# Sparse attention two heads ahead, its old keys and values fetched at once, all mixer weights loaded in 8 KB pairs, and the second tile's picks later

## The chip, the cores and the metric

The kernel runs on one core of a Trainium2 chip. The metric is the device time of one execution in microseconds (us). The engines are named as in the profile: PE is TensorE's matmul stream and PEld its weight loads, DVE is VectorE, ACT is ScalarE, POOL is GpSimd, SP is SyncE, which issues most of the DMAs.

## What is computed

One decoder block on 512 tokens of 1024 channels, all in 32-bit floats. Two token mixers run side by side on the same normed input `h`: a gated linear attention (GLA, 4 heads) and a sparse attention (DSA, 8 heads, each query keeping a part of the keys that an indexer chooses). Each has an output matrix, and a sigmoid gate by channel merges them ahead of a common output matrix. After that comes PEER, a mixer over 16,384 experts of which each token uses 8 x 16. In short:

```python
h = rmsnorm(x, norm1_g) * (1 + scale1) + shift1
gq, gk, gv, gr, glow, dq, dkv, iq, ik, iw, za, zb = split(h @ w_in)
ya = gla(gq, gk, gv, gr, glow) @ w_branch_a
yb = dsa(dq, dkv, iq, ik, iw, w_uk, w_uv) @ w_branch_b
x = x + gate1 * ((sigmoid(za) * ya + sigmoid(zb) * yb) @ w_out)
h2 = rmsnorm(x, norm2_g) * (1 + scale2) + shift2
x = x + gate2 * peer(h2)        # sum over 128 chosen experts: gelu(h2 . u_e) * gate_e * v_e
out = rmsnorm(x, final_norm_g)
```

The shifts, scales and gates come from `silu(c) @ w_ada + b_ada`, the conditioning vector.

## The kernel before

**Two halves of the tokens.** Tokens are handled in two halves of 256 (two tiles of 128 each). `mixing(0)` computes the mixers of the first half with each weight split into a high and a low part (`split`, L115: ACT casts the high part, DVE subtracts to get the low one) and three matmuls for each product; `mixing(1)` computes the second half with plain 32-bit matmuls (`plain`), one for each product at four times the time. In each half the order is: projections of the indexer and of the latent, four GLA heads (`project`, `mix_head`), the GLA's output matrix with its gate (`branch(0)`), eight DSA heads (`dsa_project`, `soften`, `attend`), `branch(1)`, the output matrix (`w_o`), and the norm that gives `h2`. After each half `scores` multiplies by PEER's query matrix and finds the best keys.

**Weights.** `raw` (L157) brings a weight of 128 x 1024 elements (4 KB to a partition, 512 KB) by a DMA on SP into one of `NRAW = 3` slots. In the second half, where no split parts are kept, the two 8 KB slots `w2` serve as four more. A DMA into a slot waits until PE (plain) or DVE (split) has finished with what lies there, and everything behind it on SP waits too. `projT` (L190) uses one weight for a 128 x 256 result, `projN` (L197) two for a result laid out the other way.

**DSA.** `dsa_project(hh)` makes the head's queries and, from the latent and the weight `w_ukv`, its keys `kk` and values `vv` of the own 256 tokens; ACT copies them out of PSUM. The first half stores them to `kvd`, one DRAM tile for each head; the second half loads them from there with two DMAs of 128 KB for each head (L603). `soften(hh)` does the logits on PE (L618), adds the position term and finds the maximum on DVE, and exponentiates on ACT; `attend(hh)` transposes the weights (L636), copies them (`pT`), and multiplies by `vv` (L640). The loop goes one head ahead:

```python
        for hh in range(8):
            cur = soft
            if hh < 7:
                soft = soften(hh + 1, *dsa_project(hh + 1))
            attend(hh, *cur, o)
```

**PEER of the first half: the gather.** The experts of tokens 0 to 255 are fetched by index from `rows` on POOL (`gather`, L1026 and after): for tile 0, 64 steps fetch two rows of u for each token and dot them with `h2n` (L1014), 64 steps fetch rows of v and add them up (L1023); for tile 1, 128 steps fetch u and v together. It is a generator that runs in the background: `pump` (L144), called at each weight, advances it at a given rate, so its instructions stand between those of the second half on DVE. At step 40 it runs `pick(1, ...)`, eight steps in which DVE turns the scores of tile 1 into indices.

**PEER of the second half: dense.** For tokens 256 to 511 all experts are computed. `dots_of` multiplies 128 experts' rows of u (`up`, two blocks a load of 1 MB) with `h2`; the first `AHEAD = 48` of these run early. `dense` then goes over 128 blocks `ib` of 128 experts: it splits a tile of v (`vb`, two blocks to a load of 1 MB, three buffers in the pool `dn`) into `vs`, does 24 matmuls of 512 columns into four accumulators, and runs a further `dots_of`. The weights by expert lie in DRAM (`gd`) and come back as `gtile`, in a buffer of `dn` or in the one of `hl`, which the early dots' `up` tiles use. `gathered(0)` and `gathered(1)` finish the gathered tiles (gate, add, norm, out), with `fx` and `fy` in raw slots.

**What sets the order.** The code is recorded, and each engine runs its instructions in the order the recording puts them; SP's DMAs are issued in order as well. Pools reuse buffers in turn, so a tile's load waits for the last reader of the buffer that it takes.

## Time and profile before

| | us |
|---|---|
| median of 3 runs (1849.02 to 1855.12) | 1853.64 |
| the profiled execution | 1861.09 |
| its span | 1859.4 |
| PE busy | 1725.0 (93%) |
| DVE busy | 1432.8 (77%) |
| ACT busy | 719.0 (39%) |
| POOL busy | 540.5 (29%) |

The DMA engines moved 573.33 MB, 308 GB/s over the span; HBM was read for 553.86 MB. In time the stages stand so: start to 44 us; mixing of the first half 44 to 345; its scores to 450; mixing of the second half 450 to 842 (GLA to about 600, `branch(0)` to 660, DSA to 735, `branch(1)` to 776, `w_o` and the norm behind it); scores of the second half to 900; early dots, picks and building of the weights to 1188; dense 1203 to 1845; end 1859. A busy share is read against the stage: idle time of an engine that nobody waits for costs nothing, and an engine that is fully busy in a stage sets its length.

### The profile page before, as it was taken

The numbers are of one execution on the slowest core, as the hardware profiler recorded it, in microseconds if no ns is written. First come the engines' busy times: TensorE is split into PE (matmuls) and PEld (weight loads), VectorE is DVE, ScalarE is ACT, GpSimd is POOL, SyncE is SP. The second block draws the span as 40 slices with busy tenths as digits, with TensorE's granted clock in tenths as the row PEclk, the third lists the DMA queues.
The fourth block names the chain that finished last, engine by engine and source line by source line (L and its number), as shares of the span: only waits on it lengthen the run. The fifth ranks groups of instructions, "written<-read, shape, count | busy, mean of one in ns | idle before, by whom it ended". The sixth has DMA issues, their size and how long they took to land.

```text
span 1859.4 us, 25034 instructions
## 1 busy us (share of the span) xinstructions
PE 1725.0 (93%) x8898; PEld 1466.6 (79%) x8898; DVE 1432.8 (77%) x2985; ACT 719.0 (39%) x1694; POOL 540.5 (29%) x459
## 2 busy tenths in 40 slices
PE   6999999989899988988999789699999999999995
PEld 3888999878667877877778678588888888888874
DVE  5797645348999868757996999388878888788887
ACT  3644465332121134102144778243333434333343
POOL 0012000001454456653431666021222222222220
PEclk9999999989998999998999889899999999999998
DMA  7757556625786799996886999699999999999983
GB/s 289 281 182 272 187 188 213 231 88 204 245 303 237 284 353 387 381 383 233 294 286 222 345 315 367 246 416 401 403 401 404 397 404 412 395 405 410 393 354 122
DMA packets 145279, 573.33 MB, mean 308 GB/s; under 512 B 14449, under 2 KB 41201, under 8 KB 111106
## 3 DMA queue, kind: packets, MB, share of 16 engines
q1 hardware_dynamic: 89858, 303.28, 44.1%
q0 software_dynamic: 55296, 268.46, 37.4%
q8 instruction: 70, 1.15, 0.2%
q14 instruction: 55, 0.45, 0.1%
HBM read 553.86 MB, written 17.83 MB: 307 GB/s over the span
## 4 chain that ended last, share of the span: by engine, by line
issue 33%; PE 29%; DVE 15%; POOL 12%; DMA 8%; ACT 2%; SPq 0%; POOLq 0%; DVEq 0%; another core or an unknown queue 0%; ACTq 0%
POOL grow L1009 11%; PE pmm L184 8%; DMA grow<-rows,ids 4%; DVE grow L1014 3%; PE pmx L184 2%; PE pmm L187 2%; PE pmm L186 2%; PE pmm L188 2%; DVE gacc L1023 2%; DMA gd<-gs 2%; PE psc L898 2%; PE ptr L898 1%; DMA adaw<-w_ada 1%; PE pmx L187 1%; PE pmx L186 1%
## 5 line engine op out<-in xcount | busy, mean ns | idle before, releaser
L1009 POOL DMA_INDIRECT grow<-rows,ids x384 | 482.9, 1258 | 838.8 <-DVE h2n L1023 451.0
L184 PE MATMUL pmm<-h2h,up 128*128 128x256 f32 x2048 | 468.4, 381 | 5.0 <-ACT kept L943 3.1
L184 PEld LDWEIGHTS pmm<-h2h,up 128*128 128x128 f32 x2048 | 385.5, 191 | 59.3 <-ACT kept L943 3.9
L1014 DVE SCALAR_TENSOR_TENSOR grow<-grow,h2n 128x1024 f32<-128x1024 f32 x256 | 310.4, 1219 | 66.5 <-DMA grow<-rows,ids 65.2
L117 DVE TENSOR_TENSOR vs<-vb,vs 128x1024 fp32r<-128x1024 f32 x128 | 156.3, 1221 | 33.1 <-ACT vs L116 32.6
L1023 DVE SCALAR_TENSOR_TENSOR gacc<-grow,dots,gacc 128x1024 f32<-128x1024 f32 x127 | 161.9, 1275 | 15.1 <-DMA grow<-rows,ids 14.0
L1023 DVE SCALAR_TENSOR_TENSOR h2n<-grow,dots,h2n 128x1024 f32<-128x1024 f32 x127 | 162.5, 1280 | 0.0
L116 ACT CAST vs<-vb 128x1024 fp32r<-128x1024 f32 x128 | 133.3, 1042 | 6.0 <-PE ptr L188 3.9
L117 DVE TENSOR_TENSOR w<-raw,w 128x1024 fp32r<-128x1024 f32 x79 | 98.0, 1240 | 45.3 <-ACT w L116 45.0
L186 PE MATMUL psc<-vs,as 128*128 128x512 f32 x256 | 114.6, 454 | 14.5 <-ACT vs L116 14.5
L187 PE MATMUL psc<-vs,as 128*128 128x512 f32 x256 | 102.7, 401 | 10.4 <-DVE vs L117 10.4
L116 ACT CAST w<-raw 128x1024 fp32r<-128x1024 f32 x79 | 82.6, 1046 | 72.9 <-PE pmm L188 32.8
L184 PE MATMUL pmm<-hh,raw 128*128 128x256 f32 x416 | 99.8, 388 | 4.3 <-DVE bsg L689 2.1
L116 ACT CAST as<-kept 128x256 fp32r<-128x256 f32 x128 | 51.3, 403 | 133.7 <-PE ptr L187 128.9
L1062 ACT ACTIVATE dots<-dots 128x1 f32<-128x1 f32 x128 | 25.8, 202 | 198.2 <-DVE grow L1014 198.1
L188 PE MATMUL psc<-vs,as 128*128 128x512 f32 x256 | 101.0, 395 | 0.0
L187 PE MATMUL ptr<-vs,as 128*128 128x512 f32 x256 | 100.6, 393 | 0.0
L188 PE MATMUL ptr<-vs,as 128*128 128x512 f32 x256 | 100.6, 393 | 0.0
L186 PE MATMUL ptr<-vs,as 128*128 128x512 f32 x256 | 99.4, 393 | 0.0
L94 POOL TENSOR_TENSOR rs<-rs,mhalf 128x1 f32<-128x1 f32 (+1 forms) x24 | 18.1, 756 | 266.5 <-DVE rs L93 266.4
L184 PEld LDWEIGHTS pmm<-hh,raw 128*128 128x128 f32 x416 | 77.9, 193 | 17.3 <-DVE bsg L689 2.5
L117 DVE TENSOR_TENSOR as<-kept,as 128x256 fp32r<-128x256 f32 x128 | 53.4, 423 | 47.0 <-ACT as L116 46.9
(377 smaller groups left out, 3527.4 us busy)
## 6 DMA issues: line engine op xcount, KB each, us to landing
up<-u_t SPq DMA_DIRECT2D x64, 1024.0 KB
vb<-v_t SPq DMA_DIRECT2D x64, 1024.0 KB
raw<-wT SPq DMA_DIRECT2D x74, 512.0 KB
adaw<-w_ada SPq DMA_DIRECT2D x20, 1024.0 KB
raw<-wN SPq DMA_DIRECT2D x32, 512.0 KB
raw<-w_br SPq DMA_DIRECT2D x32, 512.0 KB
raw<-w_pq SPq DMA_DIRECT2D x32, 512.0 KB
gd<-gs SPq DMA_DIRECT2D x16, 640.0 KB
```

What stands on the lines that cost most here:

```text
L94: nc.gpsimd.tensor_tensor(dst, dst, mhalf[:, :w], op=ALU.pow)
L116: (hi_eng or nc.scalar.copy)(hi, src)
L117: i = (eng or nc.vector).tensor_tensor(lo, src, hi.bitcast(F32), op=ALU.subtract)
L184: nc.tensor.matmul(dst, a[0], b[0], start=first, stop=last, **kw)
L186: nc.tensor.matmul(dst, a[0], b[0], start=first, stop=False, **kw)
L187: nc.tensor.matmul(dst, a[0], b[1], start=False, stop=False, **kw)
L188: nc.tensor.matmul(dst, a[1], b[0], start=False, stop=last, **kw)
L898: nc.tensor.matmul(p[:, t], pm[:, t4_ + t], qm[:, t4_ + t], start=True, stop=True)
L1009: nc.gpsimd.indirect_dma_start(out=dst, out_offset=None, in_=table, in_offset=bass.IndirectOffsetOnAxis(ap=index[0][:, r:r + 1], axis=0))
L1014: nc.vector.scalar_tensor_tensor(u, u, 1.0, h2n[i], op0=ALU.mult, op1=ALU.mult, accum_out=dots[i][:, r:r + 1])
L1023: nc.vector.scalar_tensor_tensor(gacc, v, w, gacc, op0=ALU.mult, op1=ALU.add)
L1062: nc.scalar.activation(w, w, AF.Gelu)
```

## The change

- `pair` takes the place of `raw`: every weight of the mixers and of PEER's queries comes together with the next one as 128 x 2048 elements (8 KB to a partition, 1 MB) in one DMA. The first half has `NRAW = 2` such slots; the second half takes turns between these and the two of `w2`, four in all. `w_ukv` rides with the query weight of its head (1536 columns). The host lays the weights out in these pairs.
- DSA projects two heads ahead, and `logits` (PE, DVE) is separated from `soften` (ACT), which runs after `attend` of the head before.
- `kvd` is one DRAM tile; the second half's old keys and values come in three DMAs (four heads into the buffer `hl`, twice two heads into `t4`) and are no longer copied into one tile with the new ones, so the logits of a tile are two matmuls.
- Rings: `e` from 7 to 3 buffers, and a new ring `p` of 2 for `neg`, `e2` (`enb` and `eke` together) and `pT`.
- The slabs of `w_ada` lie in rows of 8 KB; those of the first shift come as 4, 2 and 2 to a load.
- In `dense` the tiles of v take turns between the two raw slots and `dn`, which keeps two. `fx` and `fy` of a gathered tile share a raw slot. `dg` takes the buffers of `pq`.
- The picks of tile 1 run at step 72 of the gather, not at step 40.

```diff
-NRAW = 3
+NRAW = 2
-NE = 7
+NE = 3
...
-    kvd = [dr.tile([2, P, TH], F32, name=f"kvd{i}") for i in range(8)]
+    kvd = dr.tile([P, 8, 2, TH], F32, name="kvd")
...
-    def raw(src, width, plain=False):
-
-        if plain and turn[0] % (NRAW + 4) >= NRAW:
-            if not spare:
-                w = wp.tile([P, 2, D], F32, name="raw2", tag="w2", bufs=2)
-                spare.extend([w[:, 0], w[:, 1]])
-            r = spare.pop(0)[:, :width]
-        else:
-            r = wp.tile([P, D], F32, name="raw", bufs=NRAW)[:, :width]
+    def pair(src, width, plain=False):
+
         turn[0] += plain
+        tag, bufs = ("w2", 2) if plain and turn[0] % 2 else ("raw", NRAW)
+        r = wp.tile([P, 2, D], F32, name="raw", tag=tag, bufs=bufs).rearrange("p a c -> p (a c)")[:, :width]
         nc.sync.dma_start(r, src)
-        return r
+        return r[:, 0:D], r[:, D:]
...
         def dsa_project(hh):
+
+            wq, ukv = pair(w_dsa[hh], 1536, plain)
             p = pmm()
-            projT(p[:, :TH], wT[8 + hh], h)
+            projT(p[:, :TH], wq, h)
...
-            for i, t in enumerate((kk, vv)):
-                if hf == 0:
-                    nc.sync.dma_start(kvd[hh][i], t[:, own])
-                else:
-                    nc.sync.dma_start(t[:, 0:TH], kvd[hh][i])
-            return q, kk, vv
+            if hf == 0:
+                nc.sync.dma_start(kvd[:, hh], kv)
+            return q, ([] if hf == 0 else [old[hh]]) + [kv]
...
+        old = []
+        if hf:
+            for h0, n, pool, tag, bufs in ((0, 4, hp, "hl", 1), (4, 2, tp, "t4", 2), (6, 2, tp, "t4", 2)):
+                t = pool.tile([P, n, 2, TH], F32, name="old", tag=tag, bufs=bufs)
+                nc.sync.dma_start(t, kvd[:, h0:h0 + n])
+                old += [t[:, i] for i in range(n)]
...
-        soft = soften(0, *ahead)
+        soft = logits(0, *ahead)
+        soften(*soft)
+        after = dsa_project(1)
         for hh in range(8):
-            cur = soft
+            cur, nxt = soft, after
+            if hh < 6:
+                after = dsa_project(hh + 2)
             if hh < 7:
-                soft = soften(hh + 1, *dsa_project(hh + 1))
+                soft = logits(hh + 1, *nxt)
             attend(hh, *cur, o)
+            if hh < 7:
+                soften(*soft)
...
-                projT(p, wT[16 + 8 * b + d], h)
+                wz, wb = pair(w_bz[b, d], 2 * D, plain)
+                projT(p, wz, h)
...
-                vb = dn.tile([P, 2, D], F32, name="vb", bufs=3)
+                pool, tag, bufs = ((wp, "raw", NRAW), (dn, "vb", 2))[ib // 2 % 2]
+                vb = pool.tile([P, 2, D], F32, name="vb", tag=tag, bufs=bufs)
                 nc.sync.dma_start(vb, v_t[ib // 2])
...
-            if r == 40:
+            if r == 72:
                 for h0 in range(0, 8, HG):
                     yield from pick(1, h0)
```

The diff alone does not tell where the instructions come to stand. SP, from the last product-key weights of the second half to the start of the dense stage, before (the names are the destination and the source of each DMA):

```order
L167 DMA raw_7526<-w_pq 128x1024 x2
L1073 DMA fx<-x2d_90 128x1024
L937 DMA up<-u_t 128x2048 x14
...
L909 DMA gd<-gs 128x10x128
L961 DMA gtile<-gd 128x2048
L1165 DMA fing<-fin_g 128x1024
L1166 DMA gate_9538<-gated_104 128x1024
L961 DMA gtile<-gd 128x2048
L979 DMA vb<-v_t 128x2048
L937 DMA up<-u_t 128x2048
L979 DMA vb<-v_t 128x2048 x2
```

The same stretch of SP in the changed kernel:

```order
L160 DMA raw<-w_pq 128x2048 x4
L1016 DMA vb<-v_t 128x2048
L973 DMA up<-u_t 128x2048
L1016 DMA vb<-v_t 128x2048
L973 DMA up<-u_t 128x2048 x13
...
L946 DMA gd<-gs 128x10x128
L1016 DMA vb<-v_t 128x2048
L997 DMA gtile<-gd 128x2048
L1204 DMA fing<-fin_g 128x1024
L1205 DMA gate_9314<-gated_97 128x1024
L997 DMA gtile<-gd 128x2048
L973 DMA up<-u_t 128x2048
```

Two loads of v now stand right behind the product-key weights (they are those of blocks 0, 1 and 4, 5, in the raw slots) and a third, of blocks 8, 9, ahead of the gate tile; the gate tile, the gain, the gate, the second gate tile and the next u stand as before, and the load of blocks 2, 3 behind them.

SP in the DSA heads of the second half, before (`kk` and `vv` are keys and values, `wT` the queries' weights, `w_ukv` those of keys and values, `w_br` and `wT` at the end the branch's):

```order
L603 DMA kk<-kvd_98 128x256
L167 DMA raw_6412<-wT 128x1024
L603 DMA vv<-kvd_98 128x256
L167 DMA raw_6412<-w_ukv 128x512
L167 DMA raw<-wT 128x1024
L603 DMA kk<-kvd_99 128x256
L167 DMA raw<-w_ukv 128x512
L603 DMA vv<-kvd_99 128x256
```

The same stretch in the changed kernel, with the branches on both sides:

```order
L160 DMA raw<-w_bz 128x2048 x4
L753 DMA xq<-x 128x2x256
L160 DMA raw<-w_bz 128x2048 x4
L160 DMA raw<-w_dsa 128x1536 x7
L160 DMA raw<-w_bz 128x2048 x2
L973 DMA up<-u_t 128x2048
```

The loads of old keys and values are gone from this place; their three DMAs stand behind the first half's attention, its output matrix and the first product-key weights.

PE in the same heads, before (L618 the logits, L636 the transposes, L640 the product with the values, L184 a weight's matmuls, L591 and L596 the new keys and values):

```order
L591 MATMUL pmm<-cT,raw_6412 128x256 x2
L596 MATMUL pmx<-raw_6412,cT 128x128 x4
L618 MATMUL psc<-kk,q 128x384
L618 MATMUL psc<-kk,q 128x512
L636 MATMUL ptr<-ident,wide_lg 128x128 x7
L184 MATMUL pmm<-hh,raw 128x256
L640 MATMUL pout<-pT,vv 128x128 x7
L184 MATMUL pmm<-hh,raw 128x256 x7
```

And in the changed kernel:

```order
L606 MATMUL pmm<-cT,raw 128x256 x2
L611 MATMUL pmx<-raw,cT 128x128 x4
L633 MATMUL psc<-old,q 128x256
L633 MATMUL psc<-kv,q 128x128
L633 MATMUL psc<-old,q 128x256
L633 MATMUL psc<-kv,q 128x256
L655 MATMUL ptr<-ident,wide_lg 128x128 x7
L176 MATMUL pmm<-hh,raw 128x256
```

The places in the row are alike, but the logits at L633 now belong to the head before the one whose keys were made just ahead of them, and are two matmuls for each tile, one on the old keys and one on the new.

## Rows read from the trace of the kernel before

**Rows 1.** Page, part 1: busy time, share, instructions of TensorE and weight loads, VectorE, ScalarE, GpSimd.

```profile
PE 1725.0 (93%) x8898; PEld 1466.6 (79%) x8898; DVE 1432.8 (77%) x2985; ACT 719.0 (39%) x1694; POOL 540.5 (29%) x459
```

**Rows 2.** Busy time by stretch (the columns stand in its first line).

```profile
core 0: us, PE busy (x) PEld busy (x) DVE busy (x) ACT busy (x) POOL busy (x), PEclk, DMA share, GB/s
200.00:345.00 145.00, 144.51 (x1161) 140.39 (x1160) 79.08 (x137) 81.73 (x169) 1.67 (x3) 1.00 0.62 200
560.00:620.00 60.00, 56.32 (x237) 41.84 (x237) 57.73 (x205) 12.65 (x33) 21.35 (x22) 0.91 0.56 192
620.00:680.00 60.00, 58.05 (x290) 49.77 (x289) 41.00 (x81) 11.55 (x27) 34.37 (x29) 1.00 0.94 359
680.00:740.00 60.00, 49.78 (x267) 40.48 (x266) 51.13 (x98) 26.42 (x64) 34.78 (x32) 0.94 1.02 391
740.00:800.00 60.00, 57.09 (x265) 49.35 (x264) 41.67 (x71) 6.94 (x15) 36.41 (x31) 0.97 1.00 386
800.00:842.00 42.00, 32.73 (x137) 27.56 (x136) 24.20 (x39) 4.07 (x16) 19.54 (x16) 0.90 0.99 378
1300.00:1350.00 50.00, 50.00 (x227) 42.65 (x226) 42.60 (x60) 19.95 (x48) 14.66 (x11) 1.00 0.98 404
```

**Rows 3.** Timeline of TensorE, 1186 to 1217 us, at the start of the dense stage.

```profile
1185.67 2.75 PE L184 MATMUL pmm<-h2h,up 128*128 128x256 f32 x12
...
1202.95 1.22 PE L186 MATMUL psc<-vs,as 128*128 128x512 f32 x2 [14.53 <-ACT vs L116]
...
1211.73 3.61 PE L184 MATMUL pmm<-h2h,up 128*128 128x256 f32 x16
1215.00 0.58 PE L186 MATMUL psc<-vs,as 128*128 128x512 f32 x1
```

**Rows 4.** Timeline of SyncE's DMA queue, 1160 to 1215 us.

```profile
1188.46 0.33 SPq L961 DMA_DIRECT2D gtile<-gd  x1
...
1190.47 0.45 SPq L979 DMA_DIRECT2D vb<-v_t  x1
```

**Rows 5.** Waits, 640 to 842 us: us in total, times, longest.

```profile
PE psc L618 <- ACT kk L592: 6.4, 3, 4.0
```

**Rows 6.** DMA, 640 to 842 us: queues (packets, MB, share of 16 engines), issues.

```profile
q0 software_dynamic: 14025, 51.03, 65.6%
q1 hardware_dynamic: 9068, 25.16, 32.6%
...
vv<-kvd SPq DMA_DIRECT2D x7, 128.0 KB
kk<-kvd SPq DMA_DIRECT2D x6, 128.0 KB
```

**Rows 7.** Timeline of SyncE's DMA queue, 700 to 745 us.

```profile
708.12 0.54 SPq L167 DMA_DIRECT2D raw<-wT  x1
...
720.66 0.33 SPq L167 DMA_DIRECT2D raw<-w_br  x1
```

**Rows 8.** DMA, 1240 to 1800 us: the gather's queue.

```profile
q0 software_dynamic: 16190, 117.82, 51.3%
```

**Rows 9.** Timeline of TensorE around 257 us, within one weight's 24 matmuls.

```profile
256.60 0.28 PE L186 MATMUL pmm<-hh,w 128*128 128x256 f32 x1
...
258.27 0.28 PE L188 MATMUL pmm<-hh,w 128*128 128x256 f32 x1
```

**Rows 10.** Instructions that touch raw weights, 200 to 345 us: duration ns min/median/max.

```profile
L116 ACT CAST w<-raw x40: 1035/1049/1056, 199.6 to 341.7; 128x1024 fp32r<-128x1024 f32 x40
L117 DVE TENSOR_TENSOR w<-raw,w x40: 1216/1225/1229, 200.7 to 343.0; 128x1024 fp32r<-128x1024 f32 x40
```

**Rows 11.** Instructions that touch the gather's tiles, 560 to 660 us, and their idle time.

```profile
L1014 DVE SCALAR_TENSOR_TENSOR grow<-grow,h2n x30: 1198/1215/1226, 561.7 to 659.1; 128x1024 f32<-128x1024 f32 x30
...
  DVE eqc L849: 6.8, 2
```

**Rows 12.** Waits of SyncE's DMA queue, 640 to 842 us.

```profile
SPq L167 <- PE pmm L184: 86.2, 16, 11.9
```

150 lines of the change are left out of this document (92 added, 58 removed).

## The prediction

> **What bounds the kernel now.** I read four views in this order: the busy shares, the busy time by stage, the idle time of TensorE (PE) inside the stages, and the DMA queues. PE is busy for 1725.0 of 1859.4 us [rows 1], so all that can be won without doing less arithmetic is some 134 us of idle time, and the stages tell where it lies [rows 2]. In the dense stage (1300 to 1350 us) PE has no idle time at all, 50.00 of 50, while the DMA engines are at 0.98 and 404 GB/s: two resources are full there. In the second half of the first token half (200 to 345) PE is busy 144.51 of 145 with the DMA at only 0.62. From 620 to 842 us, the sparse attention, its branch and the output projection of the second token half, PE is idle for 1.95 + 10.22 + 2.91 + 9.27 = 24.4 us with the DMA at 0.94 to 1.02, some 359 to 391 GB/s. One more hole is not inside a stage but between two: 14.53 us ahead of the first dense block [rows 3]. The change touches all of these places, and the sum is made from them.
>
> The profiled execution took 1861.09 us (span 1859.4), 7.45 us above the median of the runs shown, 1853.64. I make the sum against 1861.09 and carry the result down by 7.45. A measurement of this kernel can tell about 0.3% from no change, 5.6 us.
>
> **The change, part by part.**
>
> *1. The first value tiles of the dense stage.* Today SP issues the gate tile at 1188.46, and the first tile of v follows behind it at 1190.47 [rows 4]; PE ran out of early dots at 1185.67 + 2.75 = 1188.42, and starts on the first cast only at 1202.95 [rows 3]. In the changed order the tiles for blocks 0, 1 and 4, 5 take the two slots of the raw weights and are issued right behind the last product-key weights, hundreds of microseconds earlier, so blocks 0 and 1 follow the early dots at once. But the gate tile takes the buffer that the last early dot reads, so it is still issued at about 1188.4, and behind it on SP stand the final gain, the gate, a second gate tile, the row of u that PE wants after block 1, and the tile for block 2: 1 + 0.5 + 0.5 + 1 MB, then u and v at 1 MB each. At the 404 GB/s of [rows 2], 4.2 million bytes (to the end of u) take 10.4 us and 5.2 million take 13 us, so u lands near 1199 to 1201 and v near 1202 to 1204. PE has two blocks to do, 24 matmuls of 0.227 us, 5.5 us, then waits about 5 to 7 us for u, does the 3.3 us of dots, and begins block 2 at about 1205 to 1206. Today that is 1215.00 [rows 3]. The gain read so is 9 to 10 us. Against it stands that the dense stage is full of transfers: what is moved ahead are 2 MB, and at 404 GB/s they are worth 5.2 us, so if transfers rather than PE set the pace later on, only those 5.2 us are kept. I take 6 us, nearer to the lower figure because both resources are full, with bounds of 4 and 10.
>
> *2. The sparse attention, branch and output projection of the second half.* PE waited 6.4 us in three places for the logits' keys to be copied by ScalarE [rows 5]; projecting two heads ahead puts that copy a whole head earlier, and separating logits from softening does the like for the transposes. The 13 loads of old keys and values go from here [rows 6] to the first half's end, where the DMA share was 0.62; they stood between the weights on SP, and two weights with such loads between them are issued 12.5 us apart [rows 7]. What could swallow the gain is the DMA: if the stage is bound by transfers, only fewer or cheaper transfers shorten it. The 13 loads are 1.7 MB in 1 KB rows; at the queue's price, 32.6% of 16 engines for 202 us over 25.16 MB, which is 41.9 ns per 1000 bytes and engine, they take 4.5 us. The other 23.5 MB become 8 KB rows. The gather's own rows show what that is worth: 51.03 MB in 65.6% here, mostly 4 KB rows, is 41.5 ns per 1000 bytes, and 117.82 MB in 51.3% of 560 us later, 8 KB rows, is 39.0 [rows 6, 8]. That is 6%, or 3.7 us on the weights. Together the transfers fall by 8 us, and PE's idle time by up to 20 of its 24.4 us (the rest is the chain of the norm). I take 8 us, the bound by transfers, with ends of 0 and 20: the stage's DMA share is nearest to full.
>
> The Trainium skill, "DMA: Bandwidth & Descriptors", section Bandwidth, asks for DMAs of at least 1 MiB and gives 78% of peak at 1 MB and 97% at 16 MB, which would make the pairs worth far more than 6%. The rows speak against it: 512 KB loads already run at 391 GB/s when several are in flight, so by the rule some 20 us would be won here, by the rows 8.
>
> *3. All mixer weights in pairs, and two slots in the first half.* The first half had three slots of 4 KB per partition and now has two of 8 KB. A weight takes PE 24 matmuls at 0.12 us, 2.9 us [rows 9], so a pair is 5.8 us. A slot is free when the second of its halves has been split, and the next pair must have landed in time for a cast of 1.05 and a subtraction of 1.23 [rows 10] ahead of PE: 5.8 - 2.3 = 3.5 us are left for 1 MB, which at 404 GB/s takes 2.6 us and at the 200 GB/s of that stage [rows 2] 5.2. So a pair has between 0.9 us to spare and 1.7 us too little. Some 28 pairs (8 of the GLA values, 16 of the branches, 4 of the output) have no other matmuls beside them to cover a delay. If a quarter of them come beside another 1 MB load and lose the middle of the shortfall, 0.4 us, that is 3 us, which I take; the ends are -2 and 11 (28 times 0.4). The gain side is there since a pair halves what SP issues.
>
> *4. The picks of the second tile.* They move from step 40 to step 72 of the gather. In 560 to 620 VectorE is busy 57.73 of 60 us, PE idle 3.68, at a granted clock of 0.91 [rows 2]; the fetches wait 6.8 us for the picks there [rows 11]. The dots that take their place are 1.215 us each [rows 11], 16 of them 19.4 us, so VectorE stays nearly as full, while the picks go to 620 to 680, where VectorE has 19 us free and PE 1.95 us of idle time. What is late next is a PE matmul waiting for a branch's VectorE step behind a pick. I take -2, ends -6 and 3.
>
> *5. The rest.* The index and latent weights in pairs, the first shift's slabs as three loads a half instead of eight, smaller rings for the exponentials and the moved buffers of the last gate and norm: their work lies beside PE in stages where it has 0.5 us idle in 145, or before the first matmul, where the same bytes come. What follows the last dense matmul keeps its steps. Zero; if a cover fails (a slot of the last value tiles waiting for a norm's result), one wait of up to 5 us.
>
> The sum: -6 - 8 + 3 - 2 = -13 us, 1848.1 in the profiled execution's terms, and 1840.7 as a median. **Forecast 1841 us**; its terms' bounds, not all at once, give 1830 to 1850.
>
> **The rivals.**
>
> *Only the dense start helps.* The DMA share of 1.0 in 680 to 800 speaks for it: with weights fewer slots apart the gather simply fills the holes. Parts 1 and 3 alone: -6 + 3 = -3, and half of part 2's transfers, -4: 1846.5. Against it are the waits of PE on a copy, not on a transfer [rows 5].
>
> *The change does not reach the path.* The gate tile still stands ahead of u on SP, block 2 then starts where the transfers let it, and the middle stays as it is, bound by SP's slots (it waited 86.2 us in 16 places for PE to free one [rows 12]). Gain 0 to 3: 1852.
>
> *More than the sum.* All 20 us in part 2, 10 in part 1, part 3 free: -32, 1822. For it: PE's holes are not at places where the DMA was the releaser. Against: the share of 1.0.
>
> *Slower: pairs too large for two slots.* In part 3 the deciding point is a landing 3.5 us after the slot comes free. If SP's issue and the way to memory add 2 us to the 2.6, every one of the 28 uncovered pairs is 1.1 us late, 31 us, and the rest still gives -16: +15, 1869. For it: three slots of 512 KB left PE only 0.5 us idle in 145, so nothing is known of the depth below. Against: DMA share 0.62, most pairs would find the engines free.
>
> *Slower: the gather is starved.* Weights and gather share the engines in 640 to 842, where the gather moves twice the weights' bytes. If the engines take turns by rows, an 8 KB row against a 4 KB row halves what the gather gets while weights queue: a fetch of 524 KB (8 rows on each engine at 41.5 ns per 1000 bytes, 1.4 us) then loses another 1.4 us to the longer rows. With weights queued a quarter of the time, 97 fetches (51.03 MB, [rows 6]) lose 0.35 us each, and VectorE, in order, waits for them: 34 us against the sum's 13, which gives 1875. Against: SP's weights wait for slots, not for engines [rows 12], so their queue is seldom long; hence the smallest chance.
> The Trainium skill, "DMA: Bandwidth & Descriptors", section Queues, rings and completion order, says that an engine goes round-robin between queues by packet, and drains a whole packet before it switches; no row here shows a single turn. By that rule a longer packet of the weights holds the gather back as told above.
>
> **How the numbers follow.** Forecast 0.45, only the dense start 0.18, not on the path 0.10, more than the sum 0.10, two slots too few 0.12, gather starved 0.05. Faster by over 0.3% is below 1848.1: nearly all of the forecast (0.42), half of the dense-start case (0.10) and the tenth above: 0.62. Within 0.3%: the rest of these and the third case, 0.21. Slower: the last two cases, 0.17. The range leaves out the ends of the fastest and the slowest cases: 1818 to 1862.
>
> **What would show it.** Right: block 2's first matmul at 9 to 10 us less than 26.6 us after the last early dot, a PE wait of 5 to 7 us for u between; no wait of over 1 us for a copied key; 680 to 740 with PE at 53 to 56 of 60; PE at 141 or more of 145 from 200 on. Wrong: a cast in the first half that waits for a raw weight by more than 10 us in sum (two slots), VectorE's waits for fetched rows in 640 to 842 well over what they were (starved gather), or the dense blocks losing their full 50 of 50 (the gain of part 1 given back).

## The result, and the profile after

The changed kernel took 1865.91 us (median of 9 runs, 1861.92 to 1874.86), the kernel before 1855.12 in the same comparison (median of 9, 1849.02 to 1864.91). The ratio is 1.0055, with an interval of 1.0034 to 1.0076: the change makes the kernel slower by about 10 us, where 13 us of gain were forecast. The profiled execution took 1868.25 us (span 1866.6), 2.3 us above its median.

PE, in part 1 of the page, did the same work in the same time as before [rows 1]; what grew is idle time, 144.1 us of the span where it was 134.4:

```profile
PE 1722.5 (92%) x8930; PEld 1466.7 (79%) x8930; DVE 1431.0 (77%) x2985; ACT 719.5 (39%) x1694; POOL 543.3 (29%) x459
```

Four of the stretches of [rows 2] in the changed kernel, same columns (us, busy time of PE, PEld, DVE, ACT, POOL, PEclk, DMA share, GB/s), and one at the start of the dense stage. From 663 us on the stages stand some 6 us later than before, so the middle rows cover slightly earlier work:

```profile
200.00:345.00 145.00, 144.42 (x1159) 140.27 (x1158) 78.22 (x134) 79.81 (x163) 1.71 (x3) 1.00 0.58 200
560.00:620.00 60.00, 53.42 (x239) 41.00 (x238) 56.86 (x141) 8.98 (x25) 39.87 (x36) 0.94 0.80 294
620.00:680.00 60.00, 54.44 (x259) 47.21 (x258) 41.30 (x143) 12.38 (x29) 16.85 (x16) 0.94 0.79 294
680.00:740.00 60.00, 50.81 (x293) 45.05 (x292) 44.02 (x83) 24.00 (x60) 30.37 (x26) 0.91 0.83 314
1203.00:1216.00 13.00, 2.78 (x7) 2.17 (x7) 0.43 (x1) 0.61 (x2) 0.00 (x0) 0.70 1.01 414
```

From 200 to 345 nothing is lost, so two slots of 8 KB are enough. From 560 to 680 PE loses 6.5 us more than before, and the DMA share from 620 to 680 falls from 0.94 to 0.79: POOL, which does the fetches, is busy for 39.87 of 60 us before 620 and for 16.85 of 60 behind it.

Fixed windows blur shifted stages, so I cut the execution at starts of PE's own instructions in its timeline: the same matmul by count in each kernel. Each column sums to the span within 0.1 us. The last three columns are experiments told below: the picks put back (e1), the start's slabs loaded one by one (e16), and both (e12).

| stage, us | before | changed | e1 | e16 | e12 |
|---|---|---|---|---|---|
| start to the latent's first matmul | 38.0 | 33.8 | 34.8 | 38.0 | 37.1 |
| the latent's matmuls | 39.4 | 47.5 | 47.6 | 39.2 | 39.2 |
| rest of the first half | 271.6 | 271.2 | 272.5 | 270.7 | 272.4 |
| its scores, GLA of the second half | 265.8 | 260.6 | 266.3 | 265.6 | 260.7 |
| `branch(0)` | 42.2 | 50.5 | 41.9 | 50.4 | 41.8 |
| DSA heads | 72.7 | 64.3 | 65.2 | 64.1 | 65.1 |
| `branch(1)` and half of `w_o` | 93.2 | 102.7 | 101.7 | 100.1 | 101.1 |
| to the last early dot | 365.0 | 366.9 | 367.3 | 362.7 | 362.7 |
| last early dot to dense block 8 | 57.4 | 52.3 | 51.2 | 52.6 | 51.9 |
| block 8 to the last dense matmul | 602.0 | 604.8 | 598.9 | 600.3 | 599.0 |
| end | 12.0 | 12.1 | 11.9 | 12.0 | 12.0 |

Two lines explain nothing and must be set aside. The 5 us that the fourth stage seems to gain lie wholly in the 37.1 us before the GLA, which are 32.1 in some profiles and about 37 in others, of either kernel (e1, with the same code there as the changed kernel, has 37.1). The 2.8 us lost behind block 8 aren't in e1, e16 or e12. One profile is one execution, and such a stage may differ by 5 us from the next one.

What is left: the start loses 3.8 us (77.4 to 81.2), `branch(0)` loses 8.3, the DSA heads gain 8.4 and the stage behind them loses 9.5, the dense start gains 5.1. So the time went to two places that the prediction had at -2 and 0, and one gain was given back at once.

**The start.** PE's timeline, changed kernel (columns: start, us, engine, line, operation, out<-in, count, and idle time before it with its releaser):

```profile
33.76 0.39 PE L178 MATMUL pmx<-hh,w 128*128 128x256 f32 x1 [0.33 <-DVE hh L116]
34.49 0.58 PE L179 MATMUL pmx<-hl,w 128*128 128x256 f32 x1 [0.34 <-DVE hl L117]
34.87 0.42 PE L180 MATMUL pmx<-hh,w 128*128 128x256 f32 x1
35.22 4.72 PE L358 MATMUL pmm<-h2n,sc__118 128*1 128x512 f32 x8
39.77 1.02 PE L359 MATMUL pmm<-adaacc,ones 128*1 128x512 f32 x2
```

The same place of the kernel before:

```profile
32.78 4.45 PE L352 MATMUL pmm<-adae,sc__125 128*1 128x512 f32 x10
37.07 1.02 PE L353 MATMUL pmm<-adaacc,ones 128*1 128x512 f32 x2
38.02 0.39 PE L186 MATMUL pmx<-hh,w 128*128 128x256 f32 x1
```

The last matmuls of the first shift (`pmm<-h2n` now, `pmm<-adae` before) used to stand ahead of the latent's first products. With the slabs in three loads a half, the last one comes as part of a bigger load, its matmuls are recorded three products later, and PE takes its instructions in order: it first does three products whose splits DVE has only just made, and the shift's sum (`adaacc`), on which everything behind `h` waits, starts 2.7 us later (39.77 for 37.07). The shift goes slower, too: eight matmuls take 4.72 us, where the same eight take 3.60 in e12 below.

**`branch(0)`.** PE's timeline, changed kernel, one wait:

```profile
626.73 6.02 PE L176 MATMUL pmx<-hh,raw 128*128 128x256 f32 x16 [5.56 <-DVE yp L716]
```

DVE's timeline of that wait:

```profile
616.76 0.42 DVE L716 SCALAR_TENSOR_TENSOR yp<-bsg,pmm 128x256 f32<-128x256 f32 x1
620.98 1.23 DVE L1052 SCALAR_TENSOR_TENSOR grow<-grow,h2n 128x1024 f32<-128x1024 f32 x1 [3.80 <-DMA grow<-rows,ids]
...
625.11 1.23 DVE L1052 SCALAR_TENSOR_TENSOR grow<-grow,h2n 128x1024 f32<-128x1024 f32 x1 [2.89 <-DMA grow<-rows,ids]
...
626.26 0.42 DVE L716 SCALAR_TENSOR_TENSOR yp<-bsg,pmx 128x256 f32<-128x256 f32 x1
```

It isn't a pick that holds the branch's `yp` back. Where the picks stood there are now gather steps, whose dots wait for fetched rows (3.80 and 2.89 us); `yp` stands behind them on DVE, which is in order, and PE needs the PSUM buffer that `yp` reads. Dots alone don't do it: in `branch(0)` e1 has 22 of them for the changed kernel's 18, none waits longer than 1.6 us, and PE doesn't wait. What is special is that the rows come late: fetches are issued side by side with three 1 MB weights of the branch. Changed kernel, issues from 598 to 610 us, then from 612.5 to 622 (the last number is the median time from issue to landing, in us):

```profile
grow<-rows,ids POOLq DMA_INDIRECT x6, 5.1
```

```profile
grow<-rows,ids POOLq DMA_INDIRECT x6, 11.3
```

The branch loses 8.3 us, more than the wait. The sixteen matmuls behind the wait take 6.02 us where sixteen like them take 3.61 in [rows 3], and the granted clock there is 0.61, a mean over the levels of 1.2 and 2.4 GHz; in `branch(0)` PE is busy for 44.94 us, before for 42.10.

```profile
626.00:633.00 7.00, 6.27 (x18) 5.19 (x19) 4.74 (x11) 0.21 (x1) 3.54 (x4) 0.61 1.02 417
```

The picks, by contrast, wait for no transfer. They now run at 633 to 668 us. POOL's next fetch needs a buffer that a dot behind them must free, so none is issued from 653 to 689:

```profile
689.41 1.69 POOL L1047 DMA_INDIRECT grow<-rows,ids  x1 [36.23 <-DVE grow L1052]
```

From 663.5 to 728 the DMA is at 0.69, in e1 (picks early) at 0.95. First the changed kernel, then e1:

```profile
663.50:728.00 64.50, 59.27 (x344) 52.53 (x343) 40.59 (x84) 25.39 (x63) 23.22 (x20) 0.95 0.69 253
```

```profile
663.00:728.00 65.00, 60.84 (x343) 53.59 (x342) 49.84 (x93) 27.36 (x66) 35.62 (x31) 0.95 0.95 364
```

PE gets through the DSA heads in the same 64 to 65 us either way.

**DSA heads and what follows.** No wait of PE for a copied key is left (it was 6.4 us, [rows 5]). In its place come waits for the softmax. PE, ACT and DVE in the changed kernel around 734 us:

```profile
731.10 1.23 DVE L1052 SCALAR_TENSOR_TENSOR grow<-grow,h2n 128x1024 f32<-128x1024 f32 x1 [0.60 <-DMA grow<-rows,ids]
...
733.53 0.22 DVE L645 RECIPROCAL sm<-sm 128x1 f32<-128x1 f32 x2
```

```profile
733.72 1.23 ACT L646 ACTIVATE wide_lg<-wide_lg,sm 128x384 f32<-128x384 f32 x2 [5.27 <-DVE sm L645]
```

```profile
734.39 0.90 PE L655 MATMUL ptr<-ident,wide_lg 128*128 128x128 f32 x3 [3.96 <-ACT wide_lg L646]
```

The chain reads: transposes wait for the scaled weights, these for a reciprocal, and the reciprocal stands behind the gather's dots on DVE. In `branch(1)` PE waits for `bsg` and `yp` on the same engine. The kernel before had the same three waits, of 2.9, 5.0 and 2.6 us; now they are 9.1, 5.1 and 5.5. The waits of the whole stretch (columns: total us, times, longest), changed kernel, 663 to 830:

```profile
DVE grow L1052 <- DMA grow<-rows,ids: 25.6, 17, 4.7
...
DVE gacc L1061 <- DMA grow<-rows,ids: 9.5, 6, 3.2
...
PE ptr L655 <- ACT wide_lg L646: 9.1, 2, 5.1
...
PE pmm L176 <- DVE yp L719: 5.5, 1, 5.5
...
PE pmm L176 <- DVE bsg L718: 5.1, 3, 2.9
```

Before, 657 to 823:

```profile
DVE grow L1014 <- DMA grow<-rows,ids: 30.1, 25, 5.8
...
DVE gacc L1023 <- DMA grow<-rows,ids: 10.4, 9, 1.9
```

DVE waits less for rows, 35.1 us against 40.5, though for 72 fetches where there were 83; e1, with 82, has 34.7. So the long rows of the weights don't starve the gather.

**The dense start.** SP's queue and then PE in the changed kernel, the places of [rows 4] and [rows 3]:

```profile
1197.77 0.33 SPq L997 DMA_DIRECT2D gtile<-gd  x1
1198.16 0.42 SPq L1204 DMA_DIRECT2D fing<-fin_g  x1
1198.63 0.42 SPq L1205 DMA_DIRECT2D gate<-gated  x1
1199.10 0.64 SPq L997 DMA_DIRECT2D gtile<-gd  x1
1199.78 0.44 SPq L973 DMA_DIRECT2D up<-u_t  x1
```

```profile
1213.42 6.21 PE L176 MATMUL pmm<-h2h,up 128*128 128x256 f32 x16 [10.22 <-DMA up<-u_t]
1219.28 0.58 PE L178 MATMUL psc<-vs,as 128*128 128x512 f32 x1
```

Blocks 0 and 1 follow the early dots without a gap, as predicted, and then PE waits 10.22 us for u behind 3 MB of other loads. The sixteen matmuls behind that wait take 6.21 us, again for 3.61.

### The profile page after: what moved, and what is told of

It is laid out like the page before. It is cut to its first block, busy times and chain, and to the rows that moved or that the text cites. A ratio compares the mean times of both kernels' runs of the same rounds, so it can differ in the third digit from the quotient of the medians.

```text
span 1866.6 us, 24825 instructions
## 1 busy us (share of the span) xinstructions
PE 1722.5 (92%) x8930; PEld 1466.7 (79%) x8930; DVE 1431.0 (77%) x2985; ACT 719.5 (39%) x1694; POOL 543.3 (29%) x459
## 4 chain that ended last, share of the span: by engine, by line
PE 34%; issue 30%; DVE 14%; POOL 11%; DMA 8%; ACT 2%; SPq 0%; POOLq 0%; DVEq 0%; ACTq 0%
PE pmm L176 12%; POOL grow L1047 10%; DMA grow<-rows,ids 5%; DVE grow L1052 3%; PE pmx L176 3%; PE pmm L179 2%; PE pmm L180 2%; PE pmm L178 2%; DMA gd<-gs 2%; PE psc L935 2%; DVE gacc L1061 2%; PE ptr L935 2%; PE pmx L179 1%; PE pmx L180 1%; PE pmx L178 1%
## 5 line engine op out<-in xcount | busy, mean ns | idle before, releaser
L176 PE MATMUL pmm<-h2h,up 128*128 128x256 f32 x2048 | 473.8, 384 | 17.8 <-DMA up<-u_t 13.4
L176 PEld LDWEIGHTS pmm<-h2h,up 128*128 128x128 f32 x2048 | 389.4, 193 | 74.5 <-issue 10.6
L179 PE MATMUL ptr<-vs,as 128*128 128x512 f32 x256 | 100.1, 391 | 0.0
L180 PE MATMUL ptr<-vs,as 128*128 128x512 f32 x256 | 100.1, 391 | 0.0
L116 ACT CAST as<-kept 128x256 fp32r<-128x256 f32 x128 | 51.2, 402 | 125.2 <-PE ptr L179 125.1
```

Source lines behind the costliest of these rows:

```text
L116: (hi_eng or nc.scalar.copy)(hi, src)
L176: nc.tensor.matmul(dst, a[0], b[0], start=first, stop=last, **kw)
L179: nc.tensor.matmul(dst, a[0], b[1], start=False, stop=False, **kw)
L180: nc.tensor.matmul(dst, a[1], b[0], start=False, stop=last, **kw)
```

## The experiments

All ratios are to the kernel before, run on the same chip in the same group, with 95% intervals (about 0.2% to either side). Two ratios of different groups are compared through the kernel before, so their difference is known to some 0.3%, 5 to 6 us.

### e1: the changed kernel with the picks where they were

```diff
-            if r == 72:
+            if r == 40:
```

> The changed kernel with the picks back at step 40 of the gather; all else as changed. Theory A (the picks at step 72 stand on VectorE ahead of the branch's and the attention's own steps): the PE wait of 5.56 us in the first branch goes and with it some 6 to 8 us, so the median falls to about 1858 to 1860. Rival B (the picks cost the same wherever they stand, since the gather halts for them either way): the PE wait goes, but the GLA heads lose as much, and the median stays within 2 us of 1866.

Measured: 0.9989 (0.9969 to 1.0010), median 1861.33 us. With 1.0055 for the whole change, the later picks cost 0.66%, 12 us. In its profile `branch(0)` takes 41.9 us, and between 600 and 640 PE has no wait for `yp`; what waits is POOL, for the picks, as before [rows 11]. In the waits, 600 to 640, the row now reads:

```profile
POOL grow L1047 <- DVE eqc L886: 6.8, 2, 5.8
```

### e4: the kernel before with the later picks alone

```diff
-            if r == 40:
+            if r == 72:
```

> The kernel before with one edit alone, the picks at step 72. Theory A (the late picks cost what the changed kernel loses in the first branch): slower by 5 to 8 us, 1860 to 1863. Rival B (their place does not matter): within 2 us of 1855.

Measured: 1.0020 (0.9998 to 1.0041), 1864.10 us. `branch(0)` takes 50.9 us for 42.2, the same loss as in the changed kernel, and the DSA heads behind it 67.7 for 72.7. So the loss doesn't need the other edits. What the heads gain is lost again in the stage behind them (98.2 us for 93.2), yet the median moves by 0.20%, 4 us, which can't be told from nothing. Why it moves by less than the branch loses stays open.

### e2: softening ahead of `attend`

```diff
-            attend(hh, *cur, o)
             if hh < 7:
                 soften(*soft)
+            attend(hh, *cur, o)
```

> The changed kernel, still two heads ahead, with the softening of a head recorded before the attend of the head before it, not after. Theory A (the reciprocal of the softening stands on VectorE behind dots of the gather that wait for fetched rows, so PE's transposes wait): the PE waits of 5.12 and 3.96 us ahead of the transposes fall below 2 us each, and the median falls by 4 to 9 us to 1857 to 1862. Rival B (the stretch is bound by the fetched rows, and VectorE waits for them wherever the reciprocal stands): the waits move to another PE instruction and the median falls by less than 2 us.

Measured: 1.0047 (1.0027 to 1.0066), 1871.88 us: no gain that can be told from the changed kernel's 1.0055. The DSA heads take 60.6 us instead of 64.3, `branch(1)` and half of `w_o` 107.2 instead of 102.7. The waits ahead of the transposes fall (2.7 us in all, from 9.1), and PE waits for `bsg` instead. A wait removed in the heads comes back behind them, to within a microsecond: these waits don't set the stage's length.

### e3: the dense start's first tiles of v back in `dn`

```diff
-                pool, tag, bufs = ((wp, "raw", NRAW), (dn, "vb", 2))[ib // 2 % 2]
+                pool, tag, bufs = ((dn, "vb", 2), (wp, "raw", NRAW))[ib // 2 % 2]
```

> The changed kernel with the two homes of the value tiles swapped, so that blocks 0, 1 come into the dense stage's own buffer behind the gate tile as in the kernel before, and blocks 2, 3 early. Theory A (the early tiles gain 5 us at the start of the dense stage, and keep them where PE sets the pace): block 0 starts some 14 us after the last early dot, and the median rises by 4 to 6 us to 1870 to 1872. Rival B (the dense stage is bound by its transfers, and what the start gains is given back later): the start is later by 5 us, the end by less than 2.

Measured: 1.0078 (1.0049 to 1.0106), 1876.77 us. From the last early dot to block 8 it takes 58.3 us, as before the change (57.4), and PE's first dense matmul waits again, for a cast of a tile that came behind the gate tile:

```profile
1221.73 1.22 PE L178 MATMUL psc<-vs,as 128*128 128x512 f32 x2 [16.63 <-ACT vs L116]
```

Undoing this part costs 6 us in its stage and 0.23% in the median, which alone is less than two such ratios can tell apart.

### e5: one slot of the first half freed earlier

`one_w`, the GLA's small weights, lies in a raw slot; here it lies elsewhere.

```diff
-        one_w = wp.tile([P, 2, D], F32, name="raw", tag="raw", bufs=NRAW)[:, 0]
+        one_w = t4("one_w")
```

> The changed kernel, where the first half's small weight (the indexer's keys, 4 KB) no longer takes one of the two 8 KB slots but a buffer of its own kind. Theory A (with two slots of 8 KB the pairs ahead of the first GLA head come too late): from the first matmul on a weight to the 63rd of the latent's products the kernel before took 39.4 us and the changed one 47.5; this run takes 42 to 45, and the median falls by 2 to 5 us against the changed kernel's. Rival B (that stretch is set by the casts and by PE's order, not by the slots): 47 to 48 as before, and no change.

Measured: 1.0048 (1.0030 to 1.0066), 1867.14 us. The latent's matmuls start 6.9 us later and take 40.9 us, so they end where they did (81.6 against 81.2). Two slots weren't the cause of the lost start; its end hangs on what comes ahead, the shift. A third slot of 8 KB wasn't tried.

### e6 and e11: a slower gather in the DSA heads

Both with the picks at step 40; `RATE_DSA` is the pace of the gather there. e6:

```diff
-RATE_ADA, RATE_GLA, RATE_DSA, RATE_G, RATE_DENSE = 0.4, 0.75, 0.9, 1.0, 1.05
+RATE_ADA, RATE_GLA, RATE_DSA, RATE_G, RATE_DENSE = 0.4, 0.75, 0.65, 1.0, 1.05
```

> The changed kernel with the picks at step 40 and the gather's rate in the sparse attention, its branch and its output projection lowered from 0.9 to 0.65 steps for a weight. Theory A (from 657 to 823 us the rows that the gather fetches set the pace, so that what the two heads ahead won was given back): those 166 to 167 us shrink to 150 to 158, and the gather's lag comes back as a later end of the dense stage, since its end waits for the gather, so the total moves by less than 10 us either way. Rival B (PE's and ScalarE's own chains set it): the stretch stays at 164 to 168.

Measured: 1.0018 (0.9998 to 1.0037), 1860.45 us. From the end of `branch(0)` to half of `w_o` it takes 138.9 us, where the kernel before takes 165.9, the changed one 167.0 and e1 166.9; PE is busy 141.50 of 143 us. The windows of e6, the middle and the end:

```profile
657.00:800.00 143.00, 141.50 (x763) 124.91 (x762) 98.21 (x189) 42.20 (x106) 68.98 (x60) 1.00 0.97 379
...
1800.00:1856.00 56.00, 8.61 (x36) 6.11 (x34) 44.18 (x64) 11.47 (x36) 14.43 (x12) 0.61 0.59 215
```

With fewer gather steps PE runs through and 28 us are won: about 18 of waiting, and 10 of matmul time, since the same matmuls take 137 us at a granted clock of 1.00 where they take 147 in e1 at 0.95. The gather that was put off ends 46 us after the last dense matmul (1809.9 of a span of 1855.8). So the gather's steps hold the middle, not any one wait inside the heads.

e11 has the pace at 0.84 in the same line.

> The changed kernel with the picks at step 40 and the gather's rate in the sparse attention lowered from 0.9 to 0.84. Theory A (the fetched rows set the pace of 657 to 823 us, and the end has some slack for the gather's last steps): that stretch takes 159 to 163 us instead of 167, about 2.9 us for each step moved to the end, and the end gives back less: 0.995 to 0.998 of the kernel before. Rival B (each step put off costs as much at the end as it saves): 0.998 to 1.000.

Measured: 1.0012 (0.9993 to 1.0031), 1860.14 us: not told apart from e1. Neither pace gains. The stretch takes 166.0 us where 159 to 163 were expected, so a few steps less don't shorten it. By what the gather holds the stage, its bytes or its dots' places on DVE, these runs don't settle: e1 moves 62.2 MB there in 166.9 us and e6 52.9 MB in 138.8, at nearly one rate, but e11 moves 60.2 MB in 166.0 us and the changed kernel 55.4 MB in 167.0.

### e12 and e16: the first shift's slabs one by one

The tiles stay, only each slab is its own DMA again. e16 has this edit alone, e12 has the picks at step 40 as well.

```diff
-                nc.sync.dma_start(t, w_sh[q, :, k:k + len(parts)])
+                for i in range(len(parts)):
+                    nc.sync.dma_start(t[:, i], w_sh[q, :, k + i])
```

> The changed kernel with the picks at step 40 and the first shift's slabs loaded one by one again, eight loads a half, into the same buffers. Theory A (with three loads a half PE's order puts three matmuls of the first weight ahead of the shift's, and PE stands behind them until VectorE has split the first part): the second shift is ready at about 40 us instead of 42.7, and all until the first GLA head is 2 to 3 us earlier, about that of the median too. Rival B (the two slots of 8 KB make the first 80 us late): the shift is earlier, the first GLA head is not.

Measured: 0.9971 (0.9953 to 0.9990), 1850.11 us.

> The changed kernel with the slabs one by one and nothing else. Theory A (the slabs and the picks add up): the latent's 63rd product at 76 to 77 us, and 4 to 6 us under the changed kernel, 1.002 to 1.003 of the kernel before. Rival B (the start's gain is lost in the wait behind the picks): 1.005 as the changed kernel.

Measured: 1.0013 (0.9996 to 1.0029), 1860.57 us. Against the changed kernel the slabs alone are worth 0.42% (e16), against e1 0.18% (e12): 3 to 8 us, with 4 to 6 us in the stage (the latent ends at 77.2 us in e16 for 81.2 in the changed kernel, at 76.3 in e12 for 82.4 in e1). PE's timeline of e12 has the shift first again, its eight matmuls in 3.60 us:

```profile
32.67 3.60 PE L359 MATMUL pmm<-h2n,sc__118 128*1 128x512 f32 x8
36.10 1.02 PE L360 MATMUL pmm<-adaacc,ones 128*1 128x512 f32 x2
37.05 0.39 PE L178 MATMUL pmx<-hh,w 128*128 128x256 f32 x1
```

The picks' cost by this pair is 0.42% (e16 to e12), 8 us. e12 is the changed kernel without its two losses: 0.29% faster than before.

### e13: e12 with one head ahead

The loop of the kernel before, with the rest of the change.

```diff
-        after = dsa_project(1)
         for hh in range(8):
-            cur, nxt = soft, after
-            if hh < 6:
-                after = dsa_project(hh + 2)
-            if hh < 7:
-                soft = logits(hh + 1, *nxt)
-            attend(hh, *cur, o)
+            cur = soft
             if hh < 7:
+                soft = logits(hh + 1, *dsa_project(hh + 1))
                 soften(*soft)
+            attend(hh, *cur, o)
```

> The kernel of e12 (picks at step 40, slabs one by one), with the sparse attention one head ahead and softened at once, as in the kernel before; the old keys and values are still fetched at once. Theory A (from 657 to 823 us the gather's fetched rows set the pace): the loop of the heads takes 72 to 74 us instead of 65, the branch behind it 5 to 8 less, the stretch as a whole 165 to 168, and the time is within 2 us of e12's (0.9971 of the kernel before). Rival B (two heads ahead is worth what it saves in the loop): slower than e12 by 5 to 8 us, 0.999 to 1.001.

Measured: 1.0000 (0.9980 to 1.0021), 1857.43 us. The DSA heads take 75.7 us, the stage behind them 97.7; together 173.4 where e12 has 166.2. The median points the same way (0.29%, 5 us), but the intervals overlap, and kernels with the middle of the kernel before, unchanged, had 165.9 (before, e4), 167.6 (e10), 172.3 (e8) and 173.2 (e15). Whether two heads ahead gains anything isn't settled; it is at most some 10 us.

### e7, e8: all gate tiles later

Ahead of u stood two gate tiles, the final gain and a gate, none of which the first blocks need. e7 is e1 with these put behind later tiles of v, and every further gate tile behind the tile of v before it; e8 is the kernel before with the same edit. `issue_after` keeps what is in it behind the named DMA.

```diff
-        load_g(AHEAD // 8)
+        lastv = [None]
...
-                load_g(ib // 8 + 1)
+                with tc.issue_after(lastv[0]):
+                    load_g(ib // 8 + 1)
...
-                nc.sync.dma_start(vb, v_t[ib // 2])
+                lastv[0] = nc.sync.dma_start(vb, v_t[ib // 2]).ins
+            if ib == 8:
+                with tc.issue_after(lastv[0]):
+                    nc.sync.dma_start(fing, rowb(fin_g, D))
+                    nc.sync.dma_start(gate2, gated[1])
+            if ib == 20:
+                with tc.issue_after(lastv[0]):
+                    load_g(AHEAD // 8)
```

> The changed kernel with the picks at step 40, and with the two gate tiles, the final gain and the second gate issued some blocks later, behind the first value tiles and rows of u, instead of ahead of them. Theory A (those 3 MB ahead of u on SP are what PE waits for at the start of the dense stage): the wait of about 10 us for u falls to 3 or less, and the median falls by 6 to 9 us against the run with the picks alone, to 0.994 to 0.996 of the kernel before. Rival B (the transfers are the bound and the 3 MB only come later): the wait falls, PE waits later instead, and the median falls by less than 2 us.

Measured: 1.0073 (1.0049 to 1.0096), 1871.05 us.

> The kernel before with the same edit alone: gate tiles, gain and gate issued later. Theory A: the first value tile is the first load behind the last early dot and lands some 9 us sooner; the hole of 14.5 us falls to 5 to 8, and the median falls by 6 to 9 us, to 0.995 to 0.997 of the kernel before, as much as the early tiles won without taking a slot. Rival B: less than 2 us.

Measured: 1.0066 (1.0045 to 1.0087), 1869.42 us. The start gains: 39.4 us from the last early dot to block 8 in e7 (51.2 in e1), 42.3 in e8 (57.4 before). From block 24 to block 115 it is lost again, and more: 487.2 and 491.4 us where the kernel before has 466.4. The waits of e8, 1180 to 1860, show at what: DVE weighs an expert with a gate tile that has not come.

```profile
DVE kept L973 <- DMA gtile<-gd: 37.2, 7, 9.2
```

### e9, e10, e14, e15: only the first loads later

The gate tiles of later blocks stay where they were. e9 (on e1) and e10 (on the kernel before):

```diff
-            if ib % 8 == 0:
+            if ib % 8 == 0 and ib > AHEAD:
...
+            if ib in (8, 20, 26):
+                with tc.issue_after(lastv[0]):
+                    if ib == 8:
+                        nc.sync.dma_start(fing, rowb(fin_g, D))
+                        nc.sync.dma_start(gate2, gated[1])
+                    else:
+                        load_g(AHEAD // 8 + (ib > 20))
```

> The changed kernel with the picks at step 40, and the final gain, the second gate and the first two gate tiles issued behind value tiles of the blocks 8, 20 and 26; the later gate tiles where the changed kernel has them (the run before this had pushed those back too, and VectorE waited 36.9 us for them). Theory A (what stands ahead of u on SP costs the start of the dense stage 11 us, and PE sets the pace after it): VectorE's waits for gate tiles are gone, block 2 starts about 10 us after block 0, and the median is 8 to 11 us under that of the run with the picks alone, 0.993 to 0.995 of the kernel before. Rival B (the gather and its transfers end the stage whatever PE does): the start gains 11 us, the blocks from 100 on and the end give back more than half.

Measured: 0.9987 (0.9968 to 1.0007), 1854.35 us.

> The kernel before with the same edit alone. Theory A: block 0 starts 2 us after the last early dot, and the median is 0.993 to 0.996 of the kernel before. Rival B: 0.997 to 1.000.

Measured: 0.9941 (0.9920 to 0.9962), 1846.18 us: the lowest ratio of all, with nothing of the change in it, and clear of both kernels, though not of e12, e14 and e15, whose intervals it meets. From the last early dot to block 8 it takes 42.3 us where the kernel before takes 57.4. SP's queue of e10, and its PE, at the dense start:

```profile
1165.67 0.37 SPq L937 DMA_DIRECT2D up<-u_t  x1
1166.09 1.12 SPq L979 DMA_DIRECT2D vb<-v_t  x2
```

```profile
1181.33 0.73 PE L186 MATMUL psc<-vs,as 128*128 128x512 f32 x2 [1.41 <-ACT vs L116]
```

The first tile of v is issued before the last early dots are done, not behind a gate tile that waits for them as in [rows 4], and PE waits 1.41 us where it waited 14.53 [rows 3]. Behind block 8 some of it goes back: 606.5 us to the last dense matmul, for 602.0.

In the changed kernel the same edit (e9) gains 11.8 us in the start over e1 and gives 7.9 of them back between blocks 8 and 24 (93.1 for 85.2), more at the end; as a ratio nothing is left. e14 is e12 and e15 the kernel before, both with the first gate tile behind the tile of v of block 6, the gain and the gate behind that of block 10, and the second gate tile at block 26:

```diff
+            if ib in (6, 10, 26):
+                with tc.issue_after(lastv[0]):
+                    if ib == 10:
...
+                        load_g(AHEAD // 8 + (ib > 6))
```

> The kernel of e12, and the first gate tile issued behind the value tile of block 6, gain and gate behind that of block 10, the second gate tile behind that of block 26. Theory A: no PE wait over 2 us for u, VectorE's wait for the first gate tile under 2 us, block 8 at 40 to 44 us after the last early dot instead of 52, and 0.990 to 0.993 of the kernel before. Rival B (the stage's transfers take it back): 0.995 to 0.998.

Measured: 0.9959 (0.9937 to 0.9982), 1850.42 us.

> The kernel before with the same order of gate tiles, gain and gate as e14. Theory A (the order of the loads is what counted, not the early tiles): 0.992 to 0.995 of the kernel before, within 3 us of e14. Rival B (the early tiles are worth some 5 us beyond it): e14 is ahead of this by 4 us or more.

Measured: 0.9961 (0.9944 to 0.9979), 1850.85 us. The two are alike: once the order of the loads is right, what the early tiles of v won is won without them. Both gain less than their first theory said. Why blocks 8 to 24 take 90 to 93 us in e9, e14 and e15 and 87.1 in e10 was not settled.

## Why the prediction was wrong

**Part 4, the picks: the step that failed most.** It put -2, with ends of -6 and 3, and looked for the danger in "a PE matmul waiting for a branch's VectorE step behind a pick". Measured: 8 us lost in `branch(0)` and 8 to 12 us in the medians of the changed kernel (e1, e16 to e12), 4 in the kernel before (e4), with the roles the other way round. The prediction counted how long DVE is busy, 57.73 of 60 us [rows 2] either way, and took the dots as filling the place of the picks evenly. By the traces, what counts is what an instruction may wait for: a pick has no transfer to wait for, a gather's dot has, and an in-order engine hands that wait on to the branch's `yp` and to PE. That the picks' place costs this is shown by the runs; that the late rows are the whole reason is read from the timelines.

**Part 5, "the rest", at zero: wrong.** The slabs of the first shift, "before the first matmul, where the same bytes come", cost 4 to 6 us in the stage, 3 to 8 in the medians (e12, e16). The bytes are the same, but a bigger load moves the place of its matmuls on PE behind products that come later, and the shift is on the path. The order of PE in the first 45 us would have told it; the prediction didn't look there. The wait of up to 5 us that it named as an end was of the right size, in another place.

**Part 2, the middle: direction right inside the heads, its size wrong for the stage.** Forecast -8 (0 to -20). The heads gain 8.4 us in the profiles and the stage behind them loses 9.5; the sum is 167.0 for 165.9, and from 680 to 740 PE is busy for 50.81 us where 53 to 56 was the mark. The term that failed is "the transfers fall by 8 us". The queues of 166 to 167 us of this stretch, before and then e1 (columns: packets, MB, share of 16 engines):

```profile
q0 software_dynamic: 11875, 43.21, 67.6%
q1 hardware_dynamic: 6852, 19.08, 30.1%
```

```profile
q0 software_dynamic: 11723, 42.69, 67.6%
q1 hardware_dynamic: 2888, 19.42, 29.5%
```

SP's packets fall by more than half, its bytes don't: where the old keys and values were, loads of the next stage (u, a gate) are now issued earlier, since four slots of 8 KB run further ahead. And a byte became only 3% cheaper, 0.301 x 16 x 166 / 19.08 = 41.9 ns per 1000 bytes before, 0.295 x 16 x 167 / 19.42 = 40.6 in e1; 6% were taken. The Trainium skill, "DMA: Bandwidth & Descriptors", section Bandwidth, asks for DMAs of at least 1 MiB, and the prediction's estimate by it was some 20 us; the trace doesn't agree, loads mostly of 512 KB queued behind one another already ran within 3% of loads mostly of 1 MB. What remains is the end of 0, not -8: the gather holds this stage, as e6 shows by taking steps of it away. The full transfers that the prediction named as the bound fit before and e1, but not the changed kernel itself, which moves 7 MB less in the same time.

**Part 1, the dense start: right.** Forecast -6 (-4 to -10), measured -5.1 to -6.2 in the stage (e1, e12 and the changed kernel), +6 when undone (e3). The reading of 9 to 10 us failed in two of its steps. From the gate tile's issue (1197.77) to PE's first matmul on u (1213.42) it took 15.65 us, where some 11 to 13 were read from the order, which made the wait 10.22 us rather than 5 to 7; the gather was on the same engines, at a DMA share of 1.01. And the dots behind the wait took 6.21 us, not 3.3. That the 6 us came out is in part luck: they were taken because transfers might set the pace of later blocks, and what ate the rest was this wait.

**Part 3, pairs in two slots: +3 forecast, about 0 measured.** From the end of the latent to the end of the first half it takes 271.2 us for 271.6, and from 200 to 345 PE is busy 144.42 us where 141 or more was the mark. The DMA share there is 0.58, so the argument against it, that most pairs would find the engines free, held.

**The rivals.** "Two slots too few" named the right sign and a wrong cause (e5). "Gather starved" falls with DVE's waits for rows, 34.7 us in e1 against 40.5. "Only the dense start helps" describes what is left once the picks and the slabs are put back: e12 is 0.29% faster, 5.4 us, as much as the dense start alone gains. The sum in terms of what was measured: -6 for the dense start, about 0 for the middle and the slots, +8 to +12 for the picks, +3 to +8 for the slabs; the middle of these is +9.5, against a ratio that means +10.2.

## What to carry to other kernels

Before moving a block of work on an in-order engine, ask not how busy the engine stays but what the instructions that take its place may wait for, and who stands behind them. When several loads become one, look up where their consumers now stand in the consuming engine's order, above all ahead of the first critical result. And when a stage starts late, look first at what stands ahead of its load in the queue: moving 3 MB that nobody needed yet won 0.59% in one placement (e10) and 0.39% in another (e15), where the gaining edits of this change won 0.29% together (e12).

## What the runs showed that was not expected

- Freed transfer time didn't stay free: with deeper slots the queue issued later loads earlier, and the same 62 MB went through the same 166 to 167 us (62.43 MB before, 62.24 MB in e1).
- A wait of PE cost more than its length: 2.4 and 2.6 us of slower matmuls behind the waits of 5.56 and 10.22 us. The prediction counted idle time alone, and in the middle e6 won 10 us of matmul time besides the idle time.
- The same stretch of 37 us ahead of the second half's GLA takes 32.1 us in some executions and about 37 in others, in both kernels, in this study with little between; its cause is open.
- At the start, three matmuls ahead of their time cost more than their own length. The granted clock of the first 44 us was 0.98 before, 0.84 in the changed kernel and 1.00 in e12; with the levels of 1.2 and 2.4 GHz, 0.84 is a mean over both. The changed kernel's PE had idled for three short waits for DVE and ACT right before (0.67, 0.33 and 0.34 us); e12's had one of 0.67. Windows of the changed kernel, then of e12:

```profile
0.00:44.00 44.00, 25.89 (x85) 12.37 (x85) 20.44 (x43) 13.73 (x21) 2.69 (x12) 0.84 0.78 303
```

```profile
0.00:44.00 44.00, 26.66 (x99) 14.05 (x99) 23.28 (x51) 16.50 (x25) 2.69 (x12) 1.00 0.81 303
```
